# Recurrence of the second block: four chunks of 64 tokens with head pairs on partition halves, instead of two blocks of 128

## Chip, cores and metric

The program is one kernel on one core of a Trainium2 chip. The metric is device time in microseconds (us) of one execution. "Profiled execution" below is one further run that the hardware profiler recorded; all rows of the trace come from it.

## What is computed

Two transformer blocks of two layers each, on 256 tokens of width 1024, in fp32. The change concerns one part of the second block: in each of its two layers a mixer runs three branches side by side, two softmax branches ("fox", "moba") and an RWKV-7 recurrence with 8 heads of 64 channels.

```
zf = zf + (z_prev - zf) * mu                      # r, k, v and the low-rank inputs, shifted
decay = jnp.exp(-jnp.exp(-jax.nn.softplus(-w_raw) - 0.5))
kk = kk / jnp.maximum(jnp.sqrt(jnp.sum(kk * kk, axis=-1, keepdims=True)), 1e-12)
def step(state, inp):                             # state: (heads, 64, 64), one step for each token
    sa = jnp.einsum('bhij,bhj->bhi', state, -kk_t)
    state = (state * w_t[:, :, None, :] + sa[..., None] * (kk_t * a_t)[:, :, None, :]
             + v_t[..., None] * k_t[:, :, None, :])
    return state, jnp.einsum('bhij,bhj->bhi', state, r_t)
y = concat([y_fox, rwkv(...), y_moba]) @ mix_w_out[l];  x = x + y
```

## The kernel before

The program runs twelve stages in turn; `mix_0` and `mix_1` are the sixth and tenth. In `mix`, the method `rwkv` writes the recurrence into the main lane, and two generators lie beside it: lane "f" (`rest`: projections of v, r and the gate) and lane "g" (`softmaxes`: both softmax branches, then their part of the output product). A call of `self.fill("g", n)` puts n steps of lane "g" into the program at that place. A scheduler then orders each engine's instructions, so what stands on TensorE between two steps of the recurrence is seen in its order and not in the code alone. Each lane has its own two PSUM banks: tag "acc" for most of the recurrence, "ps", "f", "g".

The 256 tokens are two blocks b of 128. Eight heads lie in four tiles t of 128 channels, two heads hh to a tile (`HALF(hh)`, 64 partitions each). The names: BE and KA are the two scaled keys, AR holds the scaled -kk (index 0) and r (index 1). `gram` forms token-by-token products (gN, gM) with 128 by 128 entries per head and block, `gram_b` the same for gB; GpSimd's `affine_select` then cuts each to its triangle. The doubling loop (pX, pY on 32 by 32 pieces, four at a time in the four row groups `GRP`) and one more step build TT, the inverse of a unit triangular matrix, for pieces of 64 tokens. Then comes the serial part: for each block R (pR, what the values and the state give), U of the first 64 tokens (pU), its effect on the second 64 (pW, added into R), U of the second 64 (pU); between the blocks the state S0 (pS). `bkt` are the keys transposed to token-major, `vt` the values (`tok_major`). At the end pY sums U, values and state through M1 and M2 (gM), and pmean begins the normalisation.

An fp32 product `nc.tensor.matmul` appears as two MATMUL rows in the trace, each with its own LDWEIGHTS (the loop of R in block 0 has 8 products, and the trace 16); a transpose is one.

## Time and profile before

| | |
|---|---|
| time, median of 3 runs | 2846.07 us (2840.44 to 2847.77) |
| profiled execution, its own time | 2838.13 us |
| span of the profiled execution | 2836.4 us |
| TensorE (PE) busy | 2761.3 us, 97% |
| VectorE (DVE) busy | 2084.9 us, 74% |
| ScalarE (ACT) busy | 1700.8 us, 60% |
| GpSimd (POOL) busy | 71.6 us, 3% |
| mean granted TensorE clock | 0.978 |

The span runs from the first to the last instruction. The mean clock is the share of the upper level: 1.00 is 2.4 GHz, 0.50 is 1.2 GHz. An end of a matmul is modelled, so that lengths of pieces of work are read here from start to start.

### The profile page before, as it was taken

How to read it: one execution, taken by the hardware profiler on the slowest of the kernel's cores; microseconds unless marked ns; L12 is line 12 of the kernel's file. 1: busy time of each engine (PE TensorE's matmuls, PEld its weight loads, DVE VectorE, ACT ScalarE, POOL GpSimd, SP SyncE). 2: the span in 40 equal slices, each digit the busy share in tenths (PEclk: the TensorE clock that was granted, in tenths of full speed). 3: DMA queues.
4: the chain of work that ended last, by engine and by line, in shares of the span. 5: the costliest groups of instructions: out<-in, count | busy, mean ns of one | idle time of the engine just before them, and what ended most of it. 6: DMA issues, size and time to landing. Idle time of an engine off the chain costs nothing. (4 is left out here: it accounts for less than half of the span.)

```text
span 2836.4 us, 44947 instructions
## 1 busy us (share of the span) xinstructions
PE 2761.3 (97%) x18031; PEld 2309.2 (81%) x18031; DVE 2084.9 (74%) x3045; ACT 1700.8 (60%) x2414; POOL 71.6 (3%) x121
## 2 busy tenths in 40 slices
PE   8999988999999999999999999999999999999999
PEld 7888886878787787878778887878888888787887
DVE  7767677888988888888887667636666667655665
ACT  5555574876777777777775555445555556344554
POOL 0010000000000000000000001100000000110000
PEclk9999998999999999999999998989999999898999
DMA  5555535999899989999995543305555555122453
GB/s 180 180 193 192 167 108 201 349 344 367 319 369 352 369 310 351 363 322 369 352 359 196 190 152 112 106 16 164 178 193 171 195 176 158 55 90 81 143 192 105
DMA packets 355705, 623.43 MB, mean 220 GB/s; under 512 B 12581, under 2 KB 187953, under 8 KB 355489
## 3 DMA queue, kind: packets, MB, share of 16 engines
q1 hardware_dynamic: 354448, 620.20, 63.2%
q8 instruction: 143, 2.34, 0.4%
q0 software_dynamic: 1040, 0.29, 0.1%
q14 instruction: 74, 0.60, 0.1%
HBM read 619.40 MB, written 1.05 MB: 219 GB/s over the span
## 5 line engine op out<-in xcount | busy, mean ns | idle before, releaser
L193 DVE TENSOR_TENSOR wl<-wt,wh 128x1024 fp32r<-128x1024 f32 x1176 | 1388.8, 1217 | 374.1 <-ACT wh L192 372.3
L192 ACT ACTIVATE wh<-wt 128x1024 fp32r<-128x1024 f32 x1176 | 1187.8, 1052 | 425.4 <-PE acc L206 93.9
L204 PE MATMUL acc<-wh,msh 128*128 128x512 f32 x544 | 213.9, 393 | 0.0
L206 PE MATMUL acc<-wh,msl 128*128 128x512 f32 x544 | 212.8, 392 | 0.0
L205 PE MATMUL acc<-wl,msh 128*128 128x512 f32 x544 | 212.1, 390 | 0.0
L205 PE MATMUL pu<-wl,xgh 128*128 128x512 f32 x448 | 179.4, 400 | 3.7 <-DVE wl L193 3.7
L204 PE MATMUL pg<-wh,xgh 128*128 128x512 f32 x448 | 176.4, 394 | 1.3 <-ACT xgh L918 1.3
L205 PE MATMUL ya<-wl,eh 128*128 128x512 f32 x448 | 177.3, 400 | 0.0
L205 PE MATMUL pg<-wl,xgh 128*128 128x512 f32 x448 | 177.0, 395 | 0.0
L204 PE MATMUL pu<-wh,xgh 128*128 128x512 f32 x448 | 175.4, 391 | 0.0
L206 PE MATMUL pu<-wh,xgl 128*128 128x512 f32 x448 | 175.3, 391 | 0.0
L206 PE MATMUL pg<-wh,xgl 128*128 128x512 f32 x448 | 175.0, 391 | 0.0
L206 PE MATMUL ya<-wh,el 128*128 128x512 f32 x448 | 173.9, 393 | 0.0
L204 PE MATMUL ya<-wh,eh 128*128 128x512 f32 x448 | 162.0, 392 | 0.0
L396 PE MATMUL pu<-hTa,wh 128*128 128x512 f32 x424 | 155.1, 399 | 0.3 <-DVE rbc L88 0.3
L396 PE MATMUL pu<-hTb,wh 128*128 128x512 f32 x424 | 154.9, 398 | 0.0
L396 PE MATMUL pg<-hTa,wh 128*128 128x512 f32 x424 | 154.6, 399 | 0.0
L396 PE MATMUL pg<-hTb,wh 128*128 128x512 f32 x424 | 154.3, 398 | 0.0
L206 PEld LDWEIGHTS acc<-wh,msl 128*128 128x128 f32 x544 | 102.1, 188 | 24.1 <-DVE msl L511 1.3
L204 PEld LDWEIGHTS acc<-wh,msh 128*128 128x128 f32 x544 | 102.1, 188 | 21.6
L397 PE MATMUL pu<-hTa,wl 128*128 128x256 f32 x424 | 119.0, 281 | 0.6 <-DVE wl L193 0.6
L397 PE MATMUL pu<-hTb,wl 128*128 128x256 f32 x424 | 119.4, 282 | 0.0
(711 smaller groups left out, 5650.2 us busy)
## 6 DMA issues: line engine op xcount, KB each, us to landing
wt<-in_moe_w_gate SPq DMA_DIRECT2D x112, 1024.0 KB, 7.3
wt<-in_moe_w_up SPq DMA_DIRECT2D x112, 1024.0 KB, 7.5
wt<-in_moe_w_down SPq DMA_DIRECT2D x112, 1024.0 KB, 6.6
wt<-in_ffn_w_in SPq DMA_DIRECT2D x88, 1024.0 KB, 5.1
wt<-in_ffn_w_out SPq DMA_DIRECT2D x44, 1024.0 KB, 5.0
wt<-in_mix_w_in SPq DMA_DIRECT2D x24, 1024.0 KB, 5.6
wt<-in_ffn_w_gate SPq DMA_DIRECT2D x14, 1024.0 KB, 5.1
wt<-in_ffn_w_up SPq DMA_DIRECT2D x14, 1024.0 KB, 5.0
```

The source lines that it names most:

```text
L192: i = nc.scalar.activation(h[:, m], t[:, s], AF.Copy)
L193: j = nc.vector.tensor_tensor(lo[:, m], t[:, s], h.bitcast(FT)[:, m], op=OP.subtract)
L204: nc.tensor.matmul(out, l[0], r[0], start=first, stop=False)
L205: nc.tensor.matmul(out, l[0], r[1], start=False, stop=False)
L206: nc.tensor.matmul(out, l[1], r[0], start=False, stop=last)
L396: mm(p, t[k][0][:, o], n.both[k], start=k == 0, stop=False)
L397: mm(p[:, :S], t[k][1][:, o], n.hT[k][0], start=False, stop=k == KT - 1)
```

## The change

The recurrence goes over four chunks c of 64 tokens. Every operand of a head now lies on that head's half of the partitions, with channels or with tokens of one chunk on it, so that every product of the recurrence is 64 by 64 with 64 columns, and the two heads of a tile follow each other on opposite halves. `gram` makes 64 by 64 triangles (and replaces `gram_b`), `headwise` replaces `tok_major` and the transposes of the keys by products with the identity, GV (gB times values) is formed for all chunks ahead of the serial part, and that part has for each chunk R (from the second chunk on), U, and S (up to the third). pW is gone; the cumulative decay starts anew at each chunk, so that its subtraction goes too. The doubling loop keeps its number and form of products.

```diff
-        cmid = self.work.tile([P, 4, 2], FT, name="cmid", tag="cmid", bufs=2)
-        cend = self.work.tile([P, 4, 2], FT, name="cend", tag="cend", bufs=2)
+        cend = self.work.tile([P, 4, 4], FT, name="cend", tag="cend", bufs=2)
         Wt, Wi, Wp = [], [], []
         for tp in range(2):
             c = self.w4("cum")
             for j in range(2):
                 V.tensor_tensor_scan(c[:, TS(j)], self.reset, sx[tp][:, TS(j)], 0.0, op0=OP.mult, op1=OP.add)
-            c4 = c.rearrange("p (t b h s) -> p t b h s", t=2, b=2, h=2)
-            cm = cmid[:, 2 * tp:2 * tp + 2, :]
-            V.tensor_copy(cm, c4[:, :, :, 0, 63])
-            V.tensor_copy(cend[:, 2 * tp:2 * tp + 2, :], c4[:, :, :, 1, 63])
-            for j in range(2):
-                V.tensor_tensor(c4[:, j, :, 0, :], c4[:, j, :, 0, :], cm[:, j, :, None].to_broadcast([P, 2, 64]), op=OP.subtract)
+            V.tensor_copy(cend[:, 2 * tp:2 * tp + 2, :], c.rearrange("p (t c s) -> p t c s", t=2, c=4)[:, :, :, 63])
...
+        def headwise(src, n, name):
+            p = self.ps("hw", tag="acc")
+            o = self.w4(name)
+            p4, o4 = (u.rearrange("p (t c i) -> p t c i", t=2, c=4) for u in (p, o))
+            for j in range(2):
+                for c in range(n):
+                    for hh in range(2):
+                        nc.tensor.matmul(p4[HALF(hh), j, c], src[HALF(hh), j * S + c * 64:j * S + c * 64 + 64],
+                                         self.ident[HALF(hh), HALF(hh)], start=True, stop=True)
+            nc.scalar.activation(o4[:, :, :n], p4[:, :, :n], AF.Copy)
+            return o4
...
-                VT.append(self.tok_major(V_[tp], 2, "vt"))
+                VT.append(headwise(V_[tp], 4, "vt"))
...
-        T2 = lambda t: (t // 2, t % 2)
         ch = lambda lst, t: lst[t // 2][:, TS(t % 2)]
-        vt = lambda t, hh, b: VT[t // 2][:, b, (t % 2) * P + hh * 64:(t % 2) * P + hh * 64 + 64]
+        part = lambda lst: (lambda t, hh, c: lst[t // 2][HALF(hh), t % 2, c])
+        vt = part(VT)
...
             res = []
...
+            for tp in range(2):
+                p = self.ps(name, tag=tag)
+                p4 = p.rearrange("p (t c s) -> p t c s", t=2, c=4)
+                for j in range(2):
+                    t = 2 * tp + j
+                    for c in range(4):
+                        for hh in range(2):
+                            nc.tensor.matmul(p4[HALF(hh), j, c], ch(lst, t)[HALF(hh), c * 64:c * 64 + 64],
+                                             AR[t][HALF(hh), c, i, :], start=True, stop=True)
+                with self.on(lane):
+                    g = self.w4(name)
+                nc.scalar.activation(g, p, AF.Copy)
+                if also:
+                    also(tp, p)
+                g8 = g.rearrange("p (n s) -> p n s", n=8)
+                for rows, base in ((P, 64), (64, 0)):
+                    nc.gpsimd.affine_select(out=g8[:rows], in_=g8[:rows], compare_op=OP.is_ge if i else OP.is_gt, fill=0.0,
+                                            base=base, pattern=[[0, 8], [1, 64]], channel_multiplier=-1)
+                res.append(g.rearrange("p (t c s) -> p t c s", t=2, c=4))
...
+            for tp in range(2):
+                px = self.ps("pX", tag=("acc", "ps")[tp])
+                for u, j, c in tb:
+                    for r, o in zip(GRP, own):
+                        nc.tensor.matmul(px[r, u * 32:u * 32 + 32], NT[tp][r, j, c, o], u3(TI[tp])[r, u], start=True, stop=True)
...
+        gb = part(gram(KA, 0, "gB"))
+        bt, kt = (part([headwise(lst[tp], 3, "bkt") for tp in range(2)]) for lst in (BE, KA))
         heads = [(t, hh) for t in range(4) for hh in range(2)]
         hs = lambda n: slice(n * 64, n * 64 + 64)
...
+        GV = []
+        for z in range(2):
+            p = self.ps("pG", tag="acc")
+            for c in range(2):
+                for t, hh in heads:
+                    nc.tensor.matmul(p[HALF(hh), hs(4 * c + t)], gb(t, hh, 2 * z + c), vt(t, hh, 2 * z + c), start=True, stop=True)
+            GV.append(self.w4("GV"))
+            nc.scalar.activation(GV[z], p, AF.Copy)
+        fac = self.work.tile([P, 4, 4, 1], FT, name="fac", tag="fac", bufs=2)
+        self.act(fac, cend[:, :, :, None], AF.Exp, scale=dec)
+        U, ST = [], [None]
+        for c in range(4):
+            R = GV[c // 2][:, c % 2 * S:c % 2 * S + S]
+            if c:
                 p = self.ps("pR", tag="acc")
...
+                for t, hh in heads:
+                    nc.tensor.matmul(p[HALF(hh), hs(t)], AR[t][HALF(hh), c, 0, :], ST[c][HALF(hh), hs(t)], start=True, stop=True)
+                V.tensor_tensor(R, p[:, :S], R, op=OP.add)
                 self.fill("g", SFILL)
...
             p = self.ps("pU", tag="acc")
...
+            for t, hh in heads:
+                nc.tensor.matmul(p[HALF(hh), hs(t)], tt(t, hh, c), R[HALF(hh), hs(t)], start=True, stop=True)
+            if c % 2 == 0:
+                Ut = self.w4("U")
+            Uc = Ut[:, c % 2 * S:c % 2 * S + S]
+            nc.scalar.activation(Uc, p[:, :S], AF.Copy)
+            U.append(Uc)
             self.fill("g", SFILL)
...
+            if c < 3:
                 p = self.ps("pS", tag="acc")
                 for t in range(4):
...
+                    for hh in range(2):
+                        nc.tensor.matmul(p[HALF(hh), hs(t)], kt(t, hh, c), vt(t, hh, c), start=True, stop=False)
+                    for hh in range(2):
+                        nc.tensor.matmul(p[HALF(hh), hs(t)], bt(t, hh, c), Uc[HALF(hh), hs(t)], start=False, stop=True)
                 S0 = self.w4("S0", 256)
...
+                v3 = lambda x_: x_.rearrange("p (t i) -> p t i", i=64)
+                last = p[:, :S]
+                if c:
+                    V.tensor_tensor(S0, last, ST[c], op=OP.add)
+                    last = S0
+                V.tensor_tensor(v3(S0), v3(last), fac[:, :, c].to_broadcast([P, 4, 64]), op=OP.mult)
+                ST.append(S0)
+                self.fill("g", SFILL)
...
-        M1, M2 = (gram(o, 1, "gM", tag="ps", lane="g") for o in (BE, KA))
+        M1, M2 = (part(gram(o, 1, "gM", tag="ps", lane="g")) for o in (BE, KA))
...
+                for c in range(4):
+                    o = [p[HALF(hh), j * S + c * 64:j * S + c * 64 + 64] for hh in range(2)]
                     for hh in range(2):
...
+                        nc.tensor.matmul(o[hh], U[c][HALF(hh), hs(t)], M1(t, hh, c), start=True, stop=False)
                     for hh in range(2):
...
+                        nc.tensor.matmul(o[hh], vt(t, hh, c), M2(t, hh, c), start=False, stop=c == 0)
+                    if c:
                         for hh in range(2):
...
+                            nc.tensor.matmul(o[hh], ST[c][HALF(hh), hs(t)], AR[t][HALF(hh), c, 1, :], start=False, stop=True)```

On TensorE, from the last products of gB to the first U of `mix_0` (gB: gram of KA; pbt: transposed keys; pR: R of block 0; pv: projections of lane "g"), before:

```order
L1575 MATMUL gB<-ar,cum 128x128 x2
L1594 MATMUL pbt<-ident,a_24399 128x128 x2
L1594 MATMUL pbt<-ident,a_24405 128x128 x2
L204 MATMUL pv<-hTb,wh 128x256
L205 MATMUL pv<-hTb,wh 128x256
L1594 MATMUL pbt<-ident,cum 128x128 x4
L1606 MATMUL pR<-vt,gB 128x64 x8
L206 MATMUL pv<-hTb,wl 128x256
```

and in the changed program, the same place (hw: `headwise` of the keys, pG: GV):

```order
L1486 MATMUL gB<-ar,cum 64x64 x15
L1422 MATMUL hw<-ident,a_24399 64x64 x12
L1422 MATMUL hw<-ident,a_24405 64x64 x12
L1422 MATMUL hw<-ident,cum 64x64 x24
L1586 MATMUL pG<-vt,gB 64x64 x32
L1602 MATMUL pU<-GV,TT 64x64 x8
L204 MATMUL pv<-hTb,wh 128x256
```

The block is one unbroken run of 64 by 64 products, and the projections of lane "g" that stood in it now stand behind the first U.

On TensorE of `mix_0`, where R of the second block is formed, before (sp, pp: scores and transposes of lane "g"; S: the state):

```order
L1575 MATMUL gB<-ar,cum 128x128 x4
L1479 MATMUL gM<-ar,a_24399 128x128
L569 MATMUL pp<-ident,at_s 128x128 x3
L545 MATMUL sp<-aq 128x128
L1575 MATMUL gB<-ar,cum 128x128 x4
L1613 MATMUL pR<-vt,gB 128x64
L1614 MATMUL pR<-S_26369,ar 128x64
```

(eight such pairs of pR follow each other, with one sp between them; then comes pU)

And in the changed program, R and U of the second chunk (acc, tm: output product and transposes of lane "g"):

```order
L1597 MATMUL pR<-S_26417,ar 64x64 x8
L204 MATMUL acc<-wh,ayh 128x512
L205 MATMUL acc<-wl,ayh 128x512
L597 MATMUL tm<-ident,av 128x128 x4
L1602 MATMUL pU<-GV,TT 64x64 x3
L545 MATMUL sp<-aq 128x128
L545 MATMUL sp<-aq 128x256
L1602 MATMUL pU<-GV,TT 64x64 x5
L545 MATMUL sp<-aq 128x128
L545 MATMUL sp<-aq 128x256
L1613 MATMUL pS<-vt,bkt 64x64 x2
L1615 MATMUL pS<-U,bkt 64x64 x2
```

The sixteen products of R that took values (128 rows) and state (64 rows) in turn are gone from here; a burst of eight products of one form stands in their place, and more steps of lane "g" lie between the bursts.

On VectorE, where the cumulative decay is formed, the difference (cum: the running sum; cmid, cend: its values at the chunk ends; w: the decay's input):

```order
-L1372 SCALAR_TENSOR_TENSOR cum<-reset,w_24387 128x256 x2
-L1375 COPY cmid<-cum 128x4
-L1376 COPY cend<-cum 128x4
-L1378 TENSOR_TENSOR cum<-cum,cmid 128x2x64 x2
-L1380 TENSOR_TENSOR w_24387<-cum,w_24387 128x512
-L1372 SCALAR_TENSOR_TENSOR cum<-reset,w_24393 128x256 x2
+L1371 SCALAR_TENSOR_TENSOR cum<-reset,w_24387 128x256 x2
+L1372 COPY cend<-cum 128x8
+L1374 TENSOR_TENSOR w_24387<-cum,w_24387 128x512
+L1371 SCALAR_TENSOR_TENSOR cum<-reset,w_24393 128x256 x2
```

Each tile pair loses one copy and two subtractions there.

## Rows read from the trace of the kernel before

**Rows 1.** The page, part 1: busy us, share of the span, instructions.
```profile
PE 2761.3 (97%) x18031; PEld 2309.2 (81%) x18031; DVE 2084.9 (74%) x3045; ACT 1700.8 (60%) x2414; POOL 71.6 (3%) x121
```
**Rows 2.** Windows: length, busy PE, PEld, DVE, ACT, POOL; granted clock, DMA, GB/s.
```profile
1843.20:1898.30 55.10, 54.78 (x430) 43.92 (x429) 11.68 (x31) 20.68 (x47) 6.93 (x11) 0.81 0.07 20
...
1863.40:1883.90 20.50, 20.50 (x100) 15.88 (x100) 4.37 (x14) 4.89 (x14) 0.00 (x0) 0.50 0.00 1
...
2519.40:2577.00 57.60, 57.28 (x433) 45.31 (x433) 11.68 (x31) 21.27 (x48) 6.93 (x11) 0.79 0.06 19
2539.20:2563.20 24.00, 24.00 (x110) 18.20 (x110) 4.79 (x14) 5.85 (x17) 0.00 (x0) 0.50 0.00 1
```
**Rows 3.** Timeline of PE, R of the second block: start, length, what.
```profile
1859.38 0.43 PE L1613 MATMUL pR<-vt,gB 128*128 128x64 f32 x2
...
1862.20 0.65 PE L545 MATMUL sp<-aq 64*128 64x256 f32 x2
```
**Rows 4.** Timeline of PE, last grams and output sum.
```profile
1888.59 3.89 PE L1479 MATMUL gM<-ar,cum 64*128 64x128 f32 x32
1892.41 0.44 PE L1660 MATMUL pY<-gM,U 128*64 128x128 f32 x4
...
1898.31 1.98 PE L1671 MATMUL pmean<-gy,bones 128*128 128x512 f32 x4
```
**Rows 5.** Timeline of PE, R of the first block and what follows.
```profile
1845.34 1.97 PE L1606 MATMUL pR<-vt,gB 128*128 128x64 f32 x16
1847.12 0.37 PE L206 MATMUL pv<-hTb,wl 128*128 128x256 f32 x1
```
**Rows 6.** Groups by line, first layer: count, busy us, mean ns, idle before.
```profile
L597 PE MATMUL tm<-ident,v 128*128 128x128 f32 x8 | 1.3, 279 | 0.0
```
**Rows 7.** Timeline of PE, first U and the step behind it.
```profile
1848.00 1.14 PE L1620 MATMUL pU<-R,TT 64*64 64x64 f32 x16
1849.07 0.38 PE L206 MATMUL pv<-hTb,wl 128*128 128x256 f32 x1
...
1849.97 0.27 PE L1625 MATMUL pW<-U,gN 64*64 64x64 f32 x1
```
**Rows 8.** Timeline of PE, the state, its two heads in turn.
```profile
1854.95 0.34 PE L1641 MATMUL pS<-U,bkt 128*64 128x64 f32 x4
1855.12 0.29 PE L1641 MATMUL pS<-vt,bkt 128*64 128x64 f32 x4
...
1855.82 0.29 PE L1641 MATMUL pS<-vt,bkt 128*64 128x64 f32 x4
1856.04 0.37 PE L1575 MATMUL gB<-ar,cum 64*128 64x128 f32 x1
```
**Rows 9.** Timeline of PE, one burst of the doubling loop.
```profile
1754.81 0.75 PE L1523 MATMUL pX<-TI,gN 32*32 32x32 f32 x64
1755.50 0.38 PE L205 MATMUL pv<-hTb,wh 128*128 128x256 f32 x1
```
**Rows 10.** Timeline of PE, state into output, heads in turn.
```profile
1893.78 0.43 PE L1665 MATMUL pY<-ar,S 64*64 64x128 f32 x4
1894.14 0.44 PE L1660 MATMUL pY<-gM,U 128*64 128x128 f32 x4
```
**Rows 11.** Timeline of PE, a gap; in brackets idle time and releaser.
```profile
1758.50 1.33 PE L1531 MATMUL pY<-X,T 32*32 32x32 f32 x108
1762.37 0.27 PE L1531 MATMUL pY<-X,T 32*32 32x32 f32 x9 [2.54 <-issue]
```
**Rows 12.** The page, part 3, queue of PE's instructions: packets, MB, share.
```profile
q8 instruction: 143, 2.34, 0.4%
```
**Rows 13.** Instructions on cmid: duration ns least, median, most; both layers.
```profile
L1378 DVE TENSOR_TENSOR cum<-cum,cmid x8: 281/284/291, 1721.7 to 2398.8; 128x128 f32<-128x128 f32 x8
```
**Rows 14.** Waits of PE, 1720 to 1740: total us, times, longest.
```profile
PE hn L463 <- DVE kksq L303: 1.5, 1, 1.5
```
**Rows 15.** Instructions on fac: duration ns least, median, most.
```profile
L1646 DVE TENSOR_TENSOR S<-pS,fac x2: 417/417/417, 1857.7 to 2534.0; 128x256 f32<-128x256 f32 x2
```

More of the change, by code (lines that the diff above doesn't have):

```diff
@@ L1392, in rwkv @@
         BE, KA, KS = [], [], []
-        AR = [self.w4("ar").rearrange("p (b i s) -> p b i s", b=2, i=2) for _ in range(4)]
+        AR = [self.w4("ar").rearrange("p (c i s) -> p c i s", c=4, i=2) for _ in range(4)]
         for tp in range(2):
@@ L1490, in gram @@
             return res
         GRP = [slice(g * 32, g * 32 + 32) for g in range(4)]
+        own = [GRP[g % 2] for g in range(4)]
         u3 = lambda x_: x_.rearrange("p (u s) -> p u s", u=8)
@@ L1553, in rwkv @@
             self.fill("f", FILL[4][0])
             self.fill("g", FILL[4][2])
-        for hh in range(2):
-            py = self.ps("pY", tag=("acc", "ps")[hh])
-            for u, t, b in tb:
-                for c in range(2):
-                    r = GRP[2 * c + 1]
-                    nc.tensor.matmul(py[GRP[2 * c], u * 32:u * 32 + 32], u3(X[hh])[r, u], u3(T2_[hh])[r, u],
+        for tp in range(2):
+            py = self.ps("pY", tag=("acc", "ps")[tp])
+            for u, j, c in tb:
+                for hh in range(2):
+                    r = GRP[2 * hh + 1]
+                    nc.tensor.matmul(py[GRP[2 * hh], u * 32:u * 32 + 32], u3(X[tp])[r, u], u3(T2_[tp])[r, u],
@@ L1561, in rwkv @@
                                      start=True, stop=True)
-            for c in range(2):
-                nc.scalar.activation(u3(TT[hh])[GRP[2 * c], :, 32:], u3(py[:, :S])[GRP[2 * c]], AF.Copy)
+            for hh in range(2):
+                nc.scalar.activation(u3(TT[tp])[GRP[2 * hh], :, 32:], u3(py[:, :S])[GRP[2 * hh]], AF.Copy)
             self.fill("f", FILL[4][1])
             self.fill("g", FILL[4][3])
+        tt = part([t_.rearrange("p (t c s) -> p t c s", t=2, c=4) for t_ in TT])
@@ L1566, in rwkv @@
         while len(VT) < 2:
             self.fill("f", 1)
-        def gram_b(b):
-            res = []
-            for hh in range(2):
-                p = self.ps("gB", tag="acc")
-                for t in range(4):
-                    nc.tensor.matmul(p[:, t * P:(t + 1) * P], ch(KA, t)[HALF(hh), b * P:(b + 1) * P],
-                                     AR[t][HALF(hh), b, 0, :], start=True, stop=True)
-                g = self.w4("gB")
-                nc.scalar.activation(g, p, AF.Copy)
-                g4 = g.rearrange("p (n s) -> p n s", n=4)
-                nc.gpsimd.affine_select(out=g4, in_=g4, compare_op=OP.is_gt, fill=0.0, base=0,
-                                        pattern=[[0, 4], [1, P]], channel_multiplier=-1)
-                res.append(g4)
-            return res
@@ L1617, in rwkv @@
-            Ub = self.w4("U")
-            p = self.ps("pU", tag="acc")
-            for n, (t, hh) in enumerate(heads):
-                nc.tensor.matmul(p[:64, hs(n)], tt(t, hh, b, 0), R[:64, hs(n)], start=True, stop=True)
-            nc.scalar.activation(Ub[:64], p[:64], AF.Copy)
-            self.fill("g", SFILL)
-            p = self.ps("pW", tag="acc")
-            for n, (t, hh) in enumerate(heads):
-                nc.tensor.matmul(p[64:, hs(n)], nt(t, hh, b)[:64, 64:], Ub[:64, hs(n)], start=True, stop=True)
@@ L1636, in rwkv @@
+            if c % 2 == 0:
[3 more added lines that the diff above has]
+            U.append(Uc)
+            self.fill("g", SFILL)
+            if c < 3:
                 p = self.ps("pS", tag="acc")
                 for t in range(4):
-                    for l_, r_, i in ((bt, lambda n: Ub[:, hs(n)], 0), (kt, lambda n: vt(n // 2, n % 2, 0), 1)):
-                        for hh in range(2):
-                            n = 2 * t + hh
-                            nc.tensor.matmul(p[HALF(hh), hs(t)], l_[0][:, hs(n)], r_(n), start=not i, stop=bool(i))
@@ L1642, in rwkv @@
[L1642 to L1648 removed]
+                    for hh in range(2):
+                        nc.tensor.matmul(p[HALF(hh), hs(t)], kt(t, hh, c), vt(t, hh, c), start=True, stop=False)
@@ new lines, in rwkv @@
+                    for hh in range(2):
+                        nc.tensor.matmul(p[HALF(hh), hs(t)], bt(t, hh, c), Uc[HALF(hh), hs(t)], start=False, stop=True)
+                S0 = self.w4("S0", 256)
+                v3 = lambda x_: x_.rearrange("p (t i) -> p t i", i=64)
[4 more added lines that the diff above has]
+                V.tensor_tensor(v3(S0), v3(last), fac[:, :, c].to_broadcast([P, 4, 64]), op=OP.mult)
```

131 lines of the change are left out of this document (28 added, 103 removed).

## The prediction

> **What bounds the kernel now.** The page comes first: TensorE is busy for 2761 of 2836 us [rows 1], so a change counts by what it takes from TensorE or lets it start sooner. The windows come next. The recurrence, from the last gB to pmean, takes 55.1 us in the first mixer and 57.6 us in the second, and TensorE is idle for 0.32 us in each [rows 2]. No other engine is near its limit there: ScalarE works 20.7 of 55.1 us, VectorE 11.7. The reader should see in the same rows that the granted clock is not 1.00: for 20.5 us of the first and 24.0 us of the second stretch it is 0.50, the lower level of 1.2 GHz. So "busy" has three contents here: streaming, the gaps between matmuls of different form, and work at half the clock. The timeline of TensorE then gives prices, each from start to start.
>
> **The work taken away, at the upper clock, for one layer.** I count MATMUL rows (two for an fp32 product).
> - Grams: 32 rows of the form 64*128 take 3.82 us [rows 4], 0.119 each. gN has 32, gB 32, gM 64: 128 rows, 15.3 us.
> - R of block 0: 16 rows, 1.78 us [rows 5].
> - R of block 1: 32 rows; 16 of them, in eight pairs that change form each time, take 2.82 us [rows 3]. Twice that is 5.64 us. (The second half ran partly at 1.2 GHz; that is counted under the clock.)
> - U, W, U of two blocks: 96 rows on one quadrant, 16 in 1.07 us [rows 7], 0.067 each: 6.4 us.
> - S: 32 rows, 1.09 us [rows 8]. Output sum: 80 rows, 5.90 us [rows 4].
> - Transposes of values and keys: 16, at 1.3 us for 8 [rows 6]: 2.6 us.
>
> Together 400 rows and 38.7 us.
>
> **The work put in.** From the loops of the change, in rows: gN 64, gB 64, gM 128, values 64, keys 96, GV 64, R 48, U 64, S 96, output 176; that is 864, all of the form 64*64 with 64 columns, the two heads on opposite halves in turn. The trace has no long run of exactly this form, so the price is bounded. From below: the state's rows in before also alternate between two halves with 64 columns, and 24 of them take 0.70 us [rows 8], 0.029 each. From above: the same form without alternation costs 0.067 [rows 7]. The nearest row is the whole block of S with its edges, 32 in 1.09 us, 0.034 each. That alternating quadrants overlap in the form 64*64 too shows in the four rows of state into output: 128 columns each, 0.36 us from start to start [rows 10], where four of 0.119 would take 0.48. I take 0.034: 29.4 us (25.2 to 57.8). The difference is -9.3 us for a layer (-13.5 to +19.1).
>
> A rule speaks against this price. Row: 64 rows of pX, four row groups into one PSUM bank, take 0.69 us [rows 9], 0.011 each. The Trainium skill, TensorEngine Tiling (Array Packing), under Restrictions and Gotchas, says that different row tiles cannot use the same PSUM bank at the same time, and here both heads write one bank. By it the pairs would run one after the other and the sum would be that of the second rival; pX, which writes other partitions of one bank from four row groups, does not agree with it.
>
> **Waits in the serial part.** Before it has nine steps (R U W U S, R U W U), afterwards ten (U S, twice R U S, R U), GV being ahead of it. A step is a burst, its evacuation and the next start: 1.97 us for U to W with a burst of 1.07 [rows 7]. With 16 rows at 0.034 the burst is 0.54, so a step is at most 1.44 us. Ten such are 14.4; three S bursts are 0.55 longer each, and two S have a second VectorE operation of 0.42 [rows 15]: 16.9 us. Its bursts are 208 rows, 7.1 us, which leaves 9.8 us for other work to cover. Other work is there: the stretch has 55.1 - 10.25 (half of the slow 20.5) = 44.9 us at the upper clock; of the 38.7 us taken away some 32 lie in it (gN 3.8, twelve gB rows 1.4 and the values 1.3 lie ahead), so about 12.7 us are lane "g" and the like. The margin is 3 us, and lane "g" is also the one whose own chain of scores, softmax and transposes waits on VectorE and ScalarE. I take +1 us a layer; nothing covered at all would be +9.8.
>
> **Instruction fetch.** The program grows by 464 rows a layer. The trace has a gap of 2.54 us that nothing releases, behind 108 rows in 1.33 us [rows 11]. PE's instructions come in 143 pieces of 16.4 KB [rows 12]; with 18031 matmuls and as many weight loads [rows 1] that is 126 matmuls a piece, an estimate. The gap fits a piece that came late. Rows with gap run at 3.87/108 = 0.036 each; the new run wants one each 0.034, so it is held up by at most 0.002 x 864 = 1.5 us if this is the pace. I take +1 us; 3.7 more pieces at 2.54 us each would be +9.4, none 0. The Trainium skill, Runtime: NRT & Kernel Launch, under Instruction fetch mechanics, calls this fetch hidden by the time that an instruction takes to issue. By that this term would be 0 and the time 2 us less; the gap speaks against it where matmuls are this short.
>
> **VectorE.** Four subtractions of 0.284 us go [rows 13], 1.1 us a layer, ahead of a point where TensorE waited 1.5 us for VectorE [rows 14]. I take -1 us (0 to -1.1). Evacuations, triangle cuts and the additions of R and S fall on engines that are idle most of the stretch [rows 2], under the same cover.
>
> Per layer: -9.3 + 1 + 1 - 1 = -8.3 us; two layers: **-16.6 us**.
>
> **The clock.** In the first mixer it is at 0.50 from 1863.4 on, directly behind the first half of R of block 1 [rows 2, 3]. What TensorE did before it fell: pairs of rows with 64 columns, a change of form behind each pair, 0.35 us a pair where the same number of rows on one quadrant takes 0.13 [rows 7]. In the second mixer the same place is in front of the fall. At 1.2 GHz, what took 44.5 us would take half: 10.25 + 12.0 = 22.2 us. The long grams and the output sum (128 and 64 columns, no form change within a run) brought no fall. In the order of the changed program the pairs are gone and what replaces them is bursts of 16 to 32 rows, but sp, pp, yp and gM lie between the bursts and each is a change of form. I judge that the clock stays at 2.4 GHz: **-22.2 us** (0 to -22.2).
>
> **Sum.** -16.6 - 22.2 = -38.8 us. On the profiled execution's own 2838.1 us that gives 2799.3 (the 1.7 us around its span stay). The median of the runs shown is 2846.1, 7.9 us (0.28%) above it, so among runs I expect 2807.
>
> **Rivals.**
> - The clock falls all the same, because the chain of bursts with lane "g" between them is again full of form changes. For: the order has more of lane "g" between the steps than before. If both stretches stay slow as long as now, only -16.6 is left: 2829. If one does: 2818.
> - Slower: the two heads' products do not overlap. Place: all 864 rows; price 0.067 instead of 0.034, +28.4 us a layer, +56.8 in all. With the clock up that is -38.8 + 56.8 = +18: 2864; with the clock down as now 2886. It decides from 0.034 + 38.8/1728 = 0.057 us a row on. Against: rows 8, 9 and 10.
> - Lane "g" doesn't cover the ten steps: +8.8 us a layer more than I took, 2825; TensorE would then be seen idle, and if that also brought the clock down, 2847, no change.
> - Fetch holds TensorE back by 2.54 us for each added piece: +8.4 us a layer more, 2824.
> - The change moves the critical work to no effect, because a wait elsewhere in the mixer takes its place: 2846. Against: 0.32 us of idle time in the stretch.
>
> **How the numbers follow.** The forecast case 0.50 (2799 to 2815); the clock falls in one or both layers 0.22 (2815 to 2832); waits or fetch eat part 0.14 (2820 to 2847); pairs not overlapping 0.07 (2855 and more); no effect 0.07. A measurement of this kernel tells a difference from none at about 0.3%, 8.5 us. Faster by more: 0.50 + 0.22 + 0.11 + 0.03 = 0.86; within: 0.05; slower 0.09. The range goes from 2795 (0.029 a row would be 8 us less than I took, and runs lie up to 5.6 us below their median) to 2832 (the clock down in both), which leaves out about 0.17.
>
> **What the profile after would show.** Runs of 64*64 rows at 0.029 to 0.036 us from start to start (0.06 and more: second rival). The stretch from the last gB to pmean near 37 us, granted clock near 1.00. TensorE idle under 1.5 us in it. Gaps "issue" behind long 64*64 runs under 0.5 us each. The wait on kksq shorter by about 1 us. I would be wrong first of all through the clock, which hangs on how closely bursts and lane "g" follow each other, and it can also change at the scores ahead of the recurrence, which the change reorders without touching them.

## The result, and the profile after

The changed kernel takes 2804.4 us (median of 4 runs, 2803.3 to 2807.6). The kernel before, run beside it, takes 2843.5 us (4 runs, 2840.4 to 2847.8). The ratio is 0.9861, 95% interval 0.9844 to 0.9877, so the change is worth 39 us. The forecast was 2807 us.

The profiled execution of the changed kernel took 2807.6 us (span 2804.8), the longest of its four; that of before took 2838.1 us. Between these two the difference is 31.6 us of span, and the rows below account for that.

The page, part 1, and of part 3 the queue of TensorE's instructions, of the changed kernel:

```profile
PE 2728.8 (97%) x18959; PEld 2289.3 (82%) x18959; DVE 2087.6 (74%) x3041; ACT 1688.5 (60%) x2380; POOL 72.0 (3%) x121
...
q8 instruction: 150, 2.46, 0.4%
```

TensorE has 928 matmul rows more than in [rows 1] (464 a layer, as counted) and is busy for 32.5 us less. Seven pieces of instructions came on top of those in [rows 12].

The windows of the recurrence, from the last gB to pmean, of the changed kernel (length, busy PE, PEld, DVE, ACT, POOL; granted clock, DMA share, GB/s):

```profile
1850.00:1887.10 37.10, 36.68 (x779) 30.49 (x777) 12.82 (x36) 16.81 (x42) 6.37 (x10) 1.00 0.10 31
2506.10:2543.20 37.10, 36.68 (x779) 30.48 (x777) 12.82 (x36) 16.81 (x42) 6.37 (x10) 1.00 0.09 31
```

Against [rows 2] the stretch falls from 55.1 to 37.1 us in the first layer. In the second it falls from 56.6 (pmean of before starts at 2576.0, 1.0 us before the window's end) to 37.1. That is -37.5 us. The granted clock is 1.00 where it was 0.81 and 0.79.

How much of this is the clock, the rows of before tell. At the upper level 16 rows on one quadrant take 1.07 us [rows 7]; the same form at the lower level, from the timeline of before:

```profile
1873.68 1.96 PE L1625 MATMUL pW<-U,gN 64*64 64x64 f32 x16
1875.58 0.79 PE L545 MATMUL sp<-aq 64*128 64x256 f32 x1
```

From start to start that is 1.90 us, 1.78 times as long and not twice. The two stretches of before agree: they hold the same work, and the second has 3.5 us more at 0.50 and is 1.5 us longer, 0.43 us for each us. So the 44.5 us at 0.50 cost about 19 us (an estimate: 0.43 of them), where the prediction took half; the other 18.5 us, some 9 a layer, are work.

The timeline of TensorE in that stretch, of the changed kernel (start, length, what; idle time and releaser in brackets):

```profile
1858.39 0.28 PE L1615 MATMUL pS<-U,bkt 64*64 64x64 f32 x4
1858.50 0.28 PE L1613 MATMUL pS<-vt,bkt 64*64 64x64 f32 x4
...
1867.80 0.68 PE L1597 MATMUL pR<-S,ar 64*64 64x64 f32 x16
1868.41 0.55 PE L569 MATMUL pp<-ident,at_s 128*128 128x128 f32 x3
...
1878.71 2.08 PE L1486 MATMUL gM<-ar,cum 64*64 64x64 f32 x64
1880.63 0.40 PE L1636 MATMUL pY<-gM,U 64*64 64x64 f32 x8
1882.07 0.33 PE L1638 MATMUL pY<-gM,vt 64*64 64x64 f32 x4 [0.38 <-POOL gM L1495]
```

From start to start, four rows of pS take 0.11 to 0.12 us (0.029 a row), 64 rows of gM 1.92 us (0.030), and 16 rows of pR 0.61 us (0.038 with the edges). Compare [rows 4], where 32 rows of gM took 3.82 us, and [rows 3], where 16 rows of pR took 2.82. The only idle time of note is 0.38 us on the triangle cut of GpSimd, and the stretch has no gap "issue".

Ahead of the recurrence the change did not do what was expected. Windows of the kernel before, from the first scan of the decays to gN and from gN to the last pg, first and second layer:

```profile
1720.20:1745.00 24.80, 21.73 (x269) 20.44 (x268) 24.43 (x65) 16.78 (x31) 5.96 (x4) 0.86 0.28 86
1745.00:1843.00 98.00, 92.79 (x1715) 76.25 (x1714) 62.98 (x137) 43.63 (x99) 12.23 (x11) 0.95 0.28 87
2394.30:2419.10 24.80, 21.14 (x270) 19.77 (x268) 24.44 (x65) 16.87 (x32) 5.92 (x4) 0.93 0.29 86
2419.10:2519.20 100.10, 95.52 (x1715) 78.33 (x1714) 62.68 (x135) 43.75 (x99) 11.26 (x11) 0.91 0.26 85
```

The same windows of the changed kernel:

```profile
1718.30:1745.90 27.60, 22.10 (x271) 21.01 (x269) 24.52 (x60) 16.71 (x32) 5.58 (x4) 0.88 0.26 77
1745.90:1849.90 104.00, 98.28 (x1823) 80.23 (x1823) 62.63 (x135) 41.48 (x87) 13.16 (x12) 0.85 0.25 82
2385.50:2411.90 26.40, 22.20 (x271) 21.02 (x269) 24.45 (x59) 16.74 (x33) 5.62 (x4) 0.87 0.26 81
2411.90:2506.10 94.20, 91.71 (x1824) 76.27 (x1823) 62.48 (x134) 41.70 (x87) 12.51 (x12) 0.95 0.29 91
```

The way to gN is longer by 2.8 and 1.6 us. The stretch with the doubling loop is longer by 6.0 us in the first layer, at a clock of 0.85 for 0.95, and shorter by 5.9 us in the second, at 0.95 for 0.91. So the account of the span is -37.5 + 4.4 + 0.1, and +1.4 us lie elsewhere.

Two more places matter for the experiments. The wait of TensorE for kksq, 1.5 us in [rows 14], is 4.2 us in the changed kernel's waits (engine line waited for: us, times, longest):

```profile
PE hn L463 <- DVE kksq L303: 4.2, 1, 4.2
```

And the gap of [rows 11] has become two in the first layer; timeline of TensorE, changed kernel:

```profile
1759.17 0.20 PE L1537 MATMUL pY<-X,T 32*32 32x32 f32 x1
...
1759.19 0.60 PE L1537 MATMUL pY<-X,T 32*32 32x32 f32 x46
1762.01 1.10 PE L1537 MATMUL pY<-X,T 32*32 32x32 f32 x80 [2.22 <-issue]
1762.91 0.86 PE L1529 MATMUL pX<-TI,gN 32*32 32x32 f32 x48
1766.03 0.43 PE L1529 MATMUL pX<-TI,gN 32*32 32x32 f32 x16 [2.27 <-issue]
```

Between the two gaps lie 80 + 48 = 128 rows.

### The profile page after: what moved, and what is told of

Its sections match the earlier page's. It is cut to its first block, busy times and chain, and to the rows that moved or that the text cites. A ratio compares the mean times of both kernels' runs of the same rounds, so it can differ in the third digit from the quotient of the medians.

```text
span 2804.8 us, 46759 instructions
## 1 busy us (share of the span) xinstructions
PE 2728.8 (97%) x18959; PEld 2289.3 (82%) x18959; DVE 2087.6 (74%) x3041; ACT 1688.5 (60%) x2380; POOL 72.0 (3%) x121
## 3 DMA queue, kind: packets, MB, share of 16 engines
q8 instruction: 150, 2.46, 0.4%
## 5 line engine op out<-in xcount | busy, mean ns | idle before, releaser
L204 PE MATMUL acc<-wh,msh 128*128 128x512 f32 x544 | 214.0, 394 | 0.0
L206 PE MATMUL acc<-wh,msl 128*128 128x512 f32 x544 | 213.3, 392 | 0.0
L205 PE MATMUL acc<-wl,msh 128*128 128x512 f32 x544 | 212.4, 390 | 0.0
L205 PE MATMUL pu<-wl,xgh 128*128 128x512 f32 x448 | 179.1, 400 | 3.7 <-DVE wl L193 3.7
L204 PE MATMUL pg<-wh,xgh 128*128 128x512 f32 x448 | 176.7, 395 | 1.3 <-ACT xgh L918 1.3
L205 PE MATMUL pg<-wl,xgh 128*128 128x512 f32 x448 | 177.7, 397 | 0.0
L205 PE MATMUL ya<-wl,eh 128*128 128x512 f32 x448 | 177.4, 400 | 0.0
L204 PE MATMUL pu<-wh,xgh 128*128 128x512 f32 x448 | 175.5, 392 | 0.0
L206 PE MATMUL pg<-wh,xgl 128*128 128x512 f32 x448 | 175.3, 391 | 0.0
L206 PE MATMUL pu<-wh,xgl 128*128 128x512 f32 x448 | 175.3, 391 | 0.0
L206 PE MATMUL ya<-wh,el 128*128 128x512 f32 x448 | 174.1, 393 | 0.0
L204 PE MATMUL ya<-wh,eh 128*128 128x512 f32 x448 | 162.1, 392 | 0.0
L206 PEld LDWEIGHTS acc<-wh,msl 128*128 128x128 f32 x544 | 102.2, 188 | 23.9 <-DVE msl L511 1.3
L204 PEld LDWEIGHTS acc<-wh,msh 128*128 128x128 f32 x544 | 102.2, 188 | 21.6
```

The source lines that it names most:

```text
L204: nc.tensor.matmul(out, l[0], r[0], start=first, stop=False)
L205: nc.tensor.matmul(out, l[0], r[1], start=False, stop=False)
L206: nc.tensor.matmul(out, l[1], r[0], start=False, stop=last)
```

## The experiments

Theory of the prediction: the alternating pairs of R of block 1 took the clock down, and products on opposite halves overlap. Rivals: the clock fell for something else in the old order, or short rows are cheap by themselves. Two questions came from the profile after: why VectorE is later, and what the gaps are. The kernel before ran beside each group of runs, with medians of 2842.6 (e1 to e4), 2843.2 (f1, f2, f3, f5) and 2843.1 us (g1, g4, f4).

| run | us, median (range) | ratio to before, 95% |
|---|---|---|
| e1_heads_in_turn | 2829.3 (2820.5 to 2836.7) | 0.9952 (0.9936 to 0.9967) |
| e2_before_state_apart | 2818.1 (2812.2 to 2827.9) | 0.9929 (0.9914 to 0.9943) |
| e3_products_on_vectore | 2792.2 (2785.8 to 2796.9) | 0.9825 (0.9809 to 0.9841) |
| e4_stream_shifted_64 | 2809.6 (2807.9 to 2810.9) | 0.9889 (0.9875 to 0.9904) |
| f1_dummy_on_gpsimd | 2806.3 (2802.6 to 2807.7) | 0.9864 (0.9846 to 0.9882) |
| f2_before_products_on_vectore | 2835.0 (2831.7 to 2838.9) | 0.9970 (0.9959 to 0.9982) |
| f3_no_lane_between_steps | 2803.9 (2800.1 to 2807.2) | 0.9858 (0.9839 to 0.9877) |
| f5_more_fill_first_round | 2801.6 (2800.0 to 2803.7) | 0.9852 (0.9834 to 0.9869) |
| g4_form_changes_added | 2868.9 (2863.1 to 2872.5) | 1.0095 (1.0077 to 1.0113) |
| g1_rope_on_vectore | 2794.5 (2792.6 to 2797.9) | 0.9832 (0.9818 to 0.9847) |
| f4_fill_spread | 2800.2 (2796.0 to 2803.7) | 0.9844 (0.9826 to 0.9862) |

### The clock: pairs taken out of before, pairs put into the changed kernel

e2, the kernel before with R of block 1 in two banks:

```diff
+                p = self.ps("pG", tag="acc")
+                for n, (t, hh) in enumerate(heads):
+                    nc.tensor.matmul(p[:, hs(n)], gb(t, hh, b), vt(t, hh, b), start=True, stop=True)
+                nc.scalar.activation(R, p, AF.Copy)
                 for hh in range(2):
                     p = self.ps("pR", tag="acc")
                     for t in range(4):
-                        nc.tensor.matmul(p[:, hs(t)], gb(t, hh, b), vt(t, hh, b), start=True, stop=False)
-                        nc.tensor.matmul(p[:, hs(t)], AR[t][HALF(hh), b, 0, :], S0[HALF(hh), hs(t)], start=False, stop=True)
-                    nc.scalar.activation(R.rearrange("p (t h i) -> p t h i", h=2, i=64)[:, :, hh],
-                                         p[:, :256].rearrange("p (t i) -> p t i", i=64), AF.Copy)
+                        nc.tensor.matmul(p[:, hs(t)], AR[t][HALF(hh), b, 0, :], S0[HALF(hh), hs(t)], start=True, stop=True)
+                    R3 = R.rearrange("p (t h i) -> p t h i", h=2, i=64)[:, :, hh]
+                    V.tensor_tensor(R3, p[:, :256].rearrange("p (t i) -> p t i", i=64), R3, op=OP.add)
```

> The kernel before, with one thing changed in R of block 1: the 16 rows of gB times values go in one run into a bank of their own and are copied out, and the 16 rows of the state follow in runs of one form, with an addition on VectorE; the eight changes of form within each half are gone. Nothing else of the change is in it. Theory of the prediction (the clock fell because of the alternating pairs): R of block 1 falls from 5.6 to about 3.7 us, the granted clock of both recurrence stretches goes from 0.78 to near 1.00, the slow stretches of 20.5 and 24 us vanish, the time falls by 4 + 22 us to about 2818. Rival (the clock fell because of what the whole order of the old recurrence did, not the pairs): the stretches stay slow for 15 us or more each, the time is 2838 to 2846.

Measured: 24.5 us less than before. Windows of the recurrence in this kernel:

```profile
1842.90:1888.40 45.50, 45.18 (x435) 36.76 (x434) 12.53 (x33) 20.30 (x46) 6.95 (x11) 1.00 0.07 25
2506.00:2551.50 45.50, 45.18 (x435) 36.78 (x434) 12.52 (x33) 20.30 (x46) 6.95 (x11) 1.00 0.07 24
```

The clock is 1.00 in both. The stretches of before without their loss at 0.50 (0.43 of 20.5 and of 24.0 us) are both 46.3 us; here they are 45.5. So this kernel saves some 0.8 us of work a layer, against the 2 us that I expected. Of the 20.7 us that the two stretches lose, about 19 are the clock; the rest of the gain lies elsewhere in the program. It is also most of what the change gained, with a few lines.

g4, the other way round, 32 pairs put into the changed kernel:

```diff
+            dum = self.ps("dum")
...
                 for t, hh in heads:
                     nc.tensor.matmul(p[HALF(hh), hs(4 * c + t)], gb(t, hh, 2 * z + c), vt(t, hh, 2 * z + c), start=True, stop=True)
+                    nc.tensor.matmul(dum[:, hs(4 * c + t)], self.bones, BE[0][:, hs(t)], start=True, stop=True)
```

> The changed kernel with one idle product of 128*128 with 64 columns behind every product of GV, into a bank that nobody reads: 32 pairs in a row that change form each time, as the 16 pairs of R of block 1 did before the change. The cost of the pairs themselves, from the 0.35 us of a pair with two rows of each form: 32 by 0.27 to 0.35 less 1.9 that GV takes now is +7 to +9 us a layer. Theory (such alternation is what brings the granted clock down): a stretch at 0.50 begins within or directly behind GV in both layers and lasts 10 to 25 us, which costs another 5 to 12 us a layer; the time is 2828 to 2846 us. Rival (the clock fell in the kernel before for something else of its order): the recurrence stays at 1.00, the time is 2818 to 2823.

Measured: 2868.9 us, over the upper end of the theory. Windows of the recurrence and of its slow part in the first layer (the second has the same lengths), then the timeline where the clock falls:

```profile
1841.40:1908.50 67.10, 66.69 (x842) 53.62 (x841) 12.81 (x36) 16.95 (x42) 6.37 (x10) 0.77 0.05 18
1849.90:1880.60 30.70, 30.70 (x158) 24.34 (x158) 0.42 (x1) 1.58 (x3) 0.00 (x0) 0.50 0.00 1
```

```profile
1848.68 0.33 PE L1587 MATMUL pG<-vt,gB 64*64 64x64 f32 x2
1848.93 0.43 PE L1588 MATMUL dum<-a,bones 128*128 128x64 f32 x2
1849.30 0.33 PE L1587 MATMUL pG<-vt,gB 64*64 64x64 f32 x2
...
1849.92 0.47 PE L1587 MATMUL pG<-vt,gB 64*64 64x64 f32 x2
...
1850.94 0.47 PE L1587 MATMUL pG<-vt,gB 64*64 64x64 f32 x2
```

The stretch grows by 30 us a layer. A pair here is two products, four rows, and takes 0.62 us at the upper clock and 1.02 at the lower. At 0.62 the 32 pairs are 19.8 us, 18 more than GV alone takes in the changed kernel (1.9); the other 12 us are the lower clock. The expectation priced the pairs at half: the 0.35 us of [rows 3] are two rows of one product with one change of form, and four rows take 0.70 there (2.82 / 4). R of block 1 has eight pairs of products, sixteen such groups of two rows. The clock falls after seven pairs in the first layer and in the sixth in the second, and stays down through the rest of them. So the pairs are needed for the fall in the old order: e2 has the same rows not in alternation, and no fall. Putting pairs in is enough for a fall in the new one (g4). No run put the same added rows into the changed kernel without alternation.

### The overlap: one head after the other

e1, in `gram`, and likewise in `headwise`, GV, R, U, S and the output sum:

```diff
-                    for c in range(4):
-                        for hh in range(2):
+                    for hh in range(2):
+                        for c in range(4):
```

> The changed kernel with the loop over the two heads of a pair outside the loop over chunks or pairs, so that runs of 64*64 rows stay on one half of the partitions (4 to 11 products in a row) in place of alternating at every product; same rows, same arithmetic. Theory (two heads on opposite halves overlap, one half alone does not): rows at 0.058 to 0.067 us in place of 0.029 to 0.032; 864 rows a layer by +0.030 are +26 us a layer, the recurrence stretch grows from 37.1 to 52 to 58 us (four gN and value rows lie ahead), the time is 2845 to 2865 us. Rival (overlap has no part in it; rows of 64 columns are cheap by themselves, and a bank that two heads share makes them wait on each other as well): rows stay at 0.029 to 0.034, the time within 0.3% of 2804.

Measured: 25 us more than the changed kernel, about midway between the two forecasts. Timeline of TensorE in e1:

```profile
1879.16 0.91 PE L1602 MATMUL pU<-GV,TT 64*64 64x64 f32 x16
1880.01 0.55 PE L569 MATMUL pp<-ident,at_s 128*128 128x128 f32 x3
...
1882.68 2.51 PE L1486 MATMUL gM<-ar,cum 64*64 64x64 f32 x61
1884.98 0.27 PE L1635 MATMUL pY<-gM,U 64*64 64x64 f32 x1
...
1888.78 0.28 PE L1635 MATMUL pY<-gM,U 64*64 64x64 f32 x2
1888.90 0.28 PE L1636 MATMUL pY<-gM,vt 64*64 64x64 f32 x2
...
1889.60 0.22 PE L1636 MATMUL pY<-gM,vt 64*64 64x64 f32 x1
1889.61 0.27 PE L1635 MATMUL pY<-gM,U 64*64 64x64 f32 x1
```

16 rows of pU, eight on either half, take 0.85 us (0.053 a row, 0.038 in the changed kernel); 61 rows of gM take 2.30 us (0.038 for 0.030). The stretch is 48.7 and 46.7 us long for 37.1; in the first layer the granted clock is 0.94 in it (it starts at the lower level), in the second 1.00, so that the second, 9.6 us longer for 702 rows, is the price of the order. The expected 52 to 58 us supposed 0.058 to 0.067 for every row. That price holds only inside a run on one half (two rows in 0.12 us at 1888.78). At a change of half the last rows and the first ones still overlap (1889.60 and 1889.61, 0.01 us apart). The rival is out: the same rows with the same arithmetic are dearer when the halves don't alternate. Two heads in one PSUM bank do work at the same time. The Trainium skill, TensorEngine Tiling (Array Packing), Restrictions and Gotchas, says that different row tiles can't use a bank at once; the alternating rows here, which write different partitions of one bank, do not agree with it (0.030 us a row of gM in the changed kernel, 0.058 inside a run on one half).

### The cover of the ten steps

f3 is one number: `SFILL = 1` becomes `SFILL = 0`.

> The changed kernel with no work of lane g put between the steps of the recurrence (the count that each step pulls goes from 1 to 0; the work follows behind the last step). Theory of the prediction (the ten serial steps hide behind lane g; uncovered they leave 9.8 us a layer idle): TensorE is idle for 7 to 10 us in each recurrence stretch, the stretch grows from 37.1 to 44 to 47 us, more if the clock falls with the idle time, the time is 2818 to 2826 us. Rival (the scheduler fills the waits with whatever is ready, wherever the code puts it): the stretch stays within 1.5 us of 37.1, the time within 0.2% of 2804.

Measured: 2803.9 us, no change; window of the recurrence, first layer (the second is as long):

```profile
1845.40:1882.80 37.40, 36.77 (x785) 30.73 (x784) 13.01 (x36) 16.77 (x42) 6.37 (x10) 1.00 0.10 31
```

The rival holds. The timeline of TensorE in f3 shows why: sp, pp, gM and yp stand between the bursts here too, because the scheduler moves work up into a wait. The cover is there, but the code between the steps is not what provides it.

### The gaps: TensorE's instructions come late

e4 repeats one transpose of 128x16 at the start of the program:

```diff
-        nc.tensor.transpose(p[:, :r], st[:r], self.ident[:r, :r])
+        [nc.tensor.transpose(p[:, :r], st[:r], self.ident[:r, :r]) for _ in range(65 if name == 'colN' else 1)]
```

> The changed kernel with 64 more transposes of 128x16 at the very start, where TensorE waits for its first loads, so that TensorE's instruction stream behind them lies 64 rows (half of 128 rows, the distance between the two unexplained gaps of the first mixer) later; the order of TensorE's instructions is otherwise the same. Theory (the gaps of 2.2 us behind short matmuls are instruction pieces that come late, at fixed places of the stream): the gaps are no longer behind row 46 of pY and 128 rows later, but 64 rows away from there, or gone, and appear elsewhere in bursts; if they go, the slow stretch of 30.7 us behind them goes or shrinks, and the time falls by up to 12 us, to 2793 to 2804. Rival (the gaps belong to the data, a wait that the profile does not show): they stay at the same row with the same 2.2 us, and the time stays within 0.1% of 2804 plus at most 3 us.

Timeline of TensorE in e4, the same place as above:

```profile
1761.19 0.20 PE L1537 MATMUL pY<-X,T 32*32 32x32 f32 x1
...
1761.22 1.28 PE L1537 MATMUL pY<-X,T 32*32 32x32 f32 x110
1765.13 0.33 PE L1537 MATMUL pY<-X,T 32*32 32x32 f32 x16 [2.64 <-issue]
```

The gap stood behind 48 rows of pY (two single ones and 46); it now stands behind 112, 64 rows further on, as many as were put in 1700 us earlier. Data cannot explain that; a boundary in the stream can. The second gap is gone from its place; two smaller ones, 1.5 us in all, stand later in the layer. The Trainium skill, Runtime: NRT & Kernel Launch, Instruction fetch mechanics, gives pieces of 256 instructions; 128 rows with 128 weight loads between two gaps agree with it. It calls their fetch mostly hidden; if the gaps are this fetch, as their place says, it costs 2.2 to 2.6 us here behind bursts of short matmuls.

The time, 2809.6 us, is 5 us above the changed kernel and outside the 2793 to 2804 of the theory: the place of the gap follows the stream, but moving it gained nothing. The stretch from gN to the last pg became 98.0 us in the first layer (104.0 before the shift) and 102.7 in the second (94.2): what one layer gained the other lost, and 2.5 us more.

### VectorE and GpSimd

e3 moves two products a pair:

```diff
-            nc.gpsimd.tensor_tensor(be, be, Wi[tp], op=OP.mult)
-            nc.gpsimd.tensor_tensor(f, f, k, op=OP.mult)
+            V.tensor_tensor(be, be, Wi[tp], op=OP.mult)
+            V.tensor_tensor(f, f, k, op=OP.mult)
```

> The changed kernel with its two large products of SBUF operands per pair (be by Wi, f by k; 128x512) on VectorE in place of GpSimd; they stand behind the key chain. Theory (small VectorE operations take 1.25 us in place of 0.16 while GpSimd runs these products, and the key chain has slid under them): the small operations go back to about 0.16 us, the wait of TensorE for kksq falls from 4.2 and 2.9 us to 1.5 or less in each layer, the time falls by 2 to 5 us to about 2800. Rival (VectorE is late because it got its inputs late or has too much to do there): the wait stays or grows by the 0.67 us of each product taken over, the time is 2804 to 2808.

Timeline of GpSimd, then of VectorE, in the changed kernel:

```profile
1732.51 1.83 POOL L1396 TENSOR_TENSOR a<-a,cum 128x512 f32<-128x512 f32 x1 [1296.12 <-ACT kf L1393]
...
1735.77 1.26 POOL L1396 TENSOR_TENSOR a<-a,cum 128x512 f32<-128x512 f32 x1 [0.17 <-ACT kf L1393]
```

```profile
1733.11 1.26 DVE L298 TENSOR_TENSOR nwt<-nwt 128x8 f32<-128x8 f32 x1
1735.77 1.28 DVE L299 SCALAR_TENSOR_TENSOR nwt<-nwt,hn_t 128x8 f32<-128x8 f32 x1
1737.05 1.75 DVE L1407 TENSOR_TENSOR cum<-kf,cum 128x512 f32<-128x512 f32 x1
```

Measured: 2792.2 us, 12 less than the changed kernel. In the changed kernel an operation on 128x8 that starts while GpSimd multiplies ends when GpSimd ends: 1733.11 + 1.26 and 1732.51 + 1.83 are both 1734.3 to 1734.4, and 1735.77 + 1.28 against 1735.77 + 1.26. In e3 the same operations take (VectorE):

```profile
1733.36 0.16 DVE L298 TENSOR_TENSOR nwt<-nwt 128x8 f32<-128x8 f32 x1
1735.54 0.68 DVE L1407 TENSOR_TENSOR cum<-kf,cum 128x512 f32<-128x512 f32 x1
```

The wait for kksq is gone, and from the first scan to gN (windows of e3):

```profile
1718.50:1739.60 21.10, 19.81 (x276) 18.98 (x274) 20.55 (x60) 16.77 (x32) 0.00 (x0) 1.00 0.33 102
...
2373.10:2394.20 21.10, 19.81 (x276) 18.93 (x275) 20.51 (x59) 16.76 (x31) 0.00 (x0) 1.00 0.32 101
```

That is 6.5 and 5.3 us less than in the changed kernel, and the clock is 1.00 there for 0.88 and 0.87. I had expected 2 to 5 us for both; 12 came, because TensorE no longer stands idle there and the clock stays up.

f1 puts two dummy products a pair back on GpSimd:

```diff
...
+            nc.scalar.activation(fs, f[:, S:S + 1], AF.Copy)
...
+            for _ in range(2):
+                nc.gpsimd.tensor_tensor(dum, Wt[tp], fs.to_broadcast([P, 512]), op=OP.mult)
             V.tensor_tensor(be, be, Wi[tp], op=OP.mult)
```

> The kernel with the products on VectorE, and beside them two GpSimd products of 128x512 a pair whose result nobody reads, started when the real ones started in the changed kernel (a one-column copy of kf on ScalarE releases them). It tells apart why moving the products gained 12 us. Theory (GpSimd's work slows VectorE's small operations, and the key chain with them): the small operations are back at about 1.25 us while the dummies run, TensorE's wait for kksq or the start of gN is again 3 to 6 us later a layer, the time is 2798 to 2808 us. Rival (the products themselves were late on GpSimd, and gN waited for their result): nobody waits for the dummies, gN starts as early as now (21.1 us behind the first scan), the time stays within 0.3% of 2792.

Measured: 2806.3 us, 14 more than e3. Scan to gN is 23.6 us (21.1 in e3), and gN itself then waits 4.2 us in its middle for VectorE (1.1 in e3), in both layers. Timeline of VectorE in f1, while the dummies run (1732.88 for 2.53 us, and 1742.95 for 2.72):

```profile
1732.97 1.54 DVE L1402 TENSOR_TENSOR kf<-kf,k 128x512 f32<-128x512 f32 x1
1734.43 1.00 DVE L299 SCALAR_TENSOR_TENSOR nwt<-nwt,hn_t 128x8 f32<-128x8 f32 x1
...
1743.52 2.44 DVE L1408 TENSOR_TENSOR ar<-kk,w 128x256 f32<-128x256 f32 x2
```

Nobody reads the dummies, so it is GpSimd's running that costs the time, and not a late result. The second pair of dummies starts 7 us later than the second pair of products did (1742.95 for 1735.77), so that another part of VectorE's chain lies under it: f1 shows the mechanism, not the same wait.

f2 is the same move in the kernel before.

> The kernel before, with the same two products on VectorE in place of GpSimd and nothing else changed. Theory (the slowing of VectorE by GpSimd was there before too, only less of the key chain lay under it: the first scan to gN took 24.9 us against 27.6 and 26.4 after the change, and 21.1 with the products moved): scan to gN falls from 24.9 to about 21 in each layer, the time by 3 to 8 us to 2835 to 2840; the slow stretches in the recurrence stay, since the pairs stay. Rival (the gain of 12 us belongs to the order that the changed kernel's scheduler made): no change, within 0.1% of 2842.6.

Measured: 8 us less (2835.0). Scan to gN is 21.3 and 22.8 us for 24.8, and the recurrence keeps its clock of 0.81 and 0.76. The cost was there before the change too.

g1 moves the two products of the rotation as well (`nc.gpsimd` to `nc.vector` in both lines).

> The kernel with the two decay products on VectorE, and the two products of the rotation (cos by q, and the sum with the turned part; 128x512) on VectorE too; TensorE's order is the same. Theory (GpSimd's products slow whatever VectorE does beside them): VectorE's chain of the scores loses its operations of over 1 us, the waits of TensorE around the rotation (0.29 and 0.15 us in each layer) shrink; there is little to gain there, 0 to 4 us: 2788 to 2792. Rival (VectorE becomes the late one, as it takes two operations of 0.67 us more on the path of q): up to 3 us slower, 2792 to 2795.

Measured: 2794.5 us. Its interval overlaps that of e3, so neither side is shown.

### Other places for the projection pieces

Both change `FILL` in e3, from ((2,2,3,1),(4,0,3,1),...): f5 to (4,2,3,1) in the first round, f4 to (2,2,3,1) in all.

> The kernel with the products on VectorE, and two more pieces of the value projection behind each half of the first doubling round (4 and 2 in place of 2 and 2), so that the bursts of short matmuls there are further apart. Theory (bursts of short matmuls in a row outrun the instruction pieces, and TensorE's idle time there is followed by stretches at half the clock: 10.2 and 6.8 us in each layer now): the gaps of 0.96, 1.84 and 1.0 us shrink, the slow stretches behind them get shorter, the time falls by 3 to 10 us to 2782 to 2789. Rival (the slow stretches come from the scores with four rows of fz between 64-row products, whatever is ahead of them): they stay, the time within 0.15% of 2792.

> The kernel with the two decay products on VectorE, with the projection pieces of lane f put 2 and 2 behind the two halves of every doubling round instead of 4 and 0 (as many in all). Theory (what brings the clock down in the doubling loop is how many short matmuls and four-row score products follow each other without wide ones between them): the slow stretches of 10.2 and 6.8 us a layer get shorter, the time falls by up to 10 us to 2782 to 2790. Rival (the scheduler had put the pieces where they were ready anyway, or another order makes other steps late, as with 4 and 2 in the first round): the time is 2790 to 2803.

Measured: 2801.6 (f5) and 2800.2 us (f4), 8 to 9 more than e3. The theory fails in both; f4 lies in its rival's range, f5 is slower than either of its forecasts. In f5 gaps "issue" of 2.5 us (one) and 2.3 us (two together) appear in the second layer where e3 had none there. In f4 the clock from gN to the last pg is 0.91 and 0.89, no better than e3's 0.91 in both. What decides the clock in the doubling loop stays open. It is not the gaps alone: e3 has 0.91 in its second layer without a gap "issue" there.

## Why the prediction was right

- **The clock, -22.2 us: right in the mechanism, 3 us too large.** The rows after show 1.00 in both stretches; e2 and g4 show the pairs as its cause. The rival "the clock falls all the same" didn't come. The size took the lower level as twice the time; the rows make it about 1.78 times, so that the term is about -19 us.
- **The price of a row, 0.034 us: right.** Inside a long run rows take 0.029 to 0.031, but with the edges, from each burst's start to the start of the next other instruction, the 702 rows of the stretch take 23.6 us in the first layer, 0.034 each. The prediction had taken its price from a block with its edges. The rival of pairs that don't overlap is refuted by the rows and by e1.
- **Work in the stretch: right in its terms, too small after them.** Of the prediction's terms, 32 of the 38.7 us taken away lie in the stretch, and 702 of the 864 rows put in (all but gN, the values and half of gB): 32 - 702 x 0.034 = 8, less 2 for waits and fetch is 6. Measured it is some 9 a layer. The terms without the 2 us come within about 1 us of that. The prediction's 12.7 us for lane "g" and the like rest on the halved clock too: with 46.3 us for the stretch at the upper level they are 14, and 37.1 - 23.6 = 13.5 after the change.
- **Waits, +1 us: too much.** Idle time is 0.42 us a stretch, 0.10 more than before. The reason was wrong in part: f3 shows that the scheduler covers the steps, wherever the code puts lane "g".
- **Fetch, +1 us: not in the stretch,** which has no gap "issue". The gaps stay in the doubling loop: 4.5 us in the first layer for 2.5 before, and 0.5 us in two in the second for 2.9.
- **VectorE, -1 us: the step that failed, in its sign.** The prediction took four subtractions away ahead of kksq and wrote that TensorE would wait about 1 us less. It waits 2.7 us longer in the first layer (4.2 for 1.5) and 0.8 in the second (2.9 for 2.1); the way to gN grew by 2.8 and 1.6 us. What the step left out is GpSimd: its products run at that place, and more of the key chain now lay under them (moving them away gains 12 us after the change, e3, and 8 before it, f2).
- **The clock ahead of the recurrence:** the prediction named it last as what could go wrong. It did, both ways: +6.0 us in one layer, -5.9 in the other.

The sum was -38.8 us. Between the medians it is -39.1; between the two profiled executions -31.6, as their times lie 5.4 us below and 3.2 us above their own medians. Which stretch differs from run to run was not looked into. That the sum meets the medians so closely is partly luck. By its terms the prediction had about -34 us in the two stretches and -4 ahead of them; the profiled executions show -37.5 there, +4.5 ahead and +1.4 elsewhere.

The fastest kernel of the study is e3, with 2792.2 us: the change and the two products on VectorE.

## What to carry to other kernels

Price a small product by its form and by what runs beside it: two heads on opposite halves of the partitions, in turn, cost about half of what they cost one after the other, and a change of form costs some 0.13 us (an estimate: 0.35 us for two rows with a change [rows 3], 0.22 for two rows of the same run [rows 5]), four times a 64 by 64 row. Where the granted clock is low, look first for rows that alternate between forms, for a run of each form alone can bring the clock back with hardly any work saved (24.5 us for a few lines here). Before costing an operation on VectorE, look at what GpSimd does at that moment.

## What the runs showed of the hardware that was not expected

- A VectorE operation of 0.16 us takes up to 1.28 us beside a product on GpSimd, and both end together. The Trainium skill, SBUF — State Buffer, Who interferes with whom, says that a VectorE operation with two SBUF inputs contends with a GpSimd operation that reads SBUF, calls the shared ports an exclusive lock, and says that the order of issue decides who blocks. The ends of the rows above agree with it.
- Work does not take twice as long at half the granted clock: 16 rows on one quadrant take 1.07 us at 1.00 and 1.90 at 0.50, 1.78 times; a pair that changes form 0.62 and 1.02 us, 1.65 times (g4). Why is not shown.
- The gap of late instructions is tied to a place in the stream: 64 rows put in at the start moved it by 64 rows, and changed which layer paid (e4).
